# One transformer block with 32 experts: the second weights on a DMA queue of their own

## The chip, the cores and the metric

The kernel runs on one core of a Trainium2 chip. Its time is the device time of one execution in microseconds (us). The engines that matter are TensorE (PE), VectorE (DVE), ScalarE (ACT), GpSimd (POOL) and SyncE (SP, which only issues transfers); 16 DMA engines move data between the memory and the core.

## The reference

One block on 256 tokens of width 1024, all in f32: a modulated mixer (forgetting attention, gated linear attention and pooling side by side), a norm, and a mixture of 32 experts of which each token takes 4, then a last norm. The experts hold nearly all of the bytes: for each expert 1024 x 2048 first weights (gate and up) and 1024 x 1024 second weights (down), 12.6 MB, 403 MB for the 32.

```python
logits = hf @ w_router + b_router
top_logit, top_e = lax.top_k(logits, TOP_K)
gate = jax.nn.softmax(top_logit, axis=-1)
...
def expert_block(args):                       # each expert on the tokens that chose it
    xb, e = args
    gu = xb @ w_gate_up[e] + b_gate_up[e]
    return clamped_swiglu(gu) @ w_down[e] + b_down[e]
...
y = y_rows[dest] * gate
x = layer_norm(DEEPNORM_ALPHA * x + (1.0 + gate2) * y, ln2_g[l], ln2_b[l])
```

## The kernel before

The mixer and the routing take the first 187 us or so; then the experts follow. Each expert has 64 slots for tokens, and two experts make a pair, whose 128 slots fill the partitions.

**Weights.** A ring of 8 slots of 128 x 4096 f32 (2.097 MB each; two pools of 5 and 3 slots) takes the tiles in turn. Expert e has four tiles `g{e}_0` to `g{e}_3` of first weights (`load_up`, L735 to 738) and two tiles `d{e}_0` and `d{e}_1` of second weights (`load_down`, L740 to 743). `load_last` (L745 to 753) brings the second weights of expert 31 in six smaller transfers. The list `jobs` sets the turn: the first weights of e, then the second weights of e - 1; `load_next` takes one. A load may be issued once the tile that stood in its slot has been read by PE, eight tiles earlier: `d0_0` takes the slot of `g0_0`, `d1_0` that of `g1_2`, `g3_0` that of `d0_0`. All of these loads stand in SP's instruction stream and go to one DMA queue.

**One pair.** `dispatch` gathers the tokens with a one-hot matrix on PE (`pxg`), and DVE and ACT scale the result into `xg` (L793 and L791). `gate_up` multiplies `xg` by the four g tiles into `gu`; DVE and ACT make the activation of it (`g` L827, the sigmoid `s` L831 on ACT, `l`). `turned` transposes it (`paT` L839 on PE, `aT` L841 on DVE). `down_sums` multiplies it by the two d tiles into `py`, DVE scales that into `yb` (L857), and `combine` adds the rows of a pair back to the tokens: `ya` on PE, with the gates `sg` (L805, transposed by PE as `psg`, L803). The `py` of an expert is written behind the gate-up of the next.

**Order.** All engines' instructions are put in order by a scheduler, from the program as written. The order on each engine is then fixed, and an engine waits at an instruction until what it needs is there. `mm` at L134 records nearly all matmuls, so that they share one line.

**The barrier.** Ahead of expert 12 the program reads a count and branches (`more_slots`, L868 to 870), for the case that an expert has more than 64 tokens; it isn't taken here. All engines branch, and SP waits there until the loads in flight have landed.

**The end.** `py30` makes `yh` (L998), and `ya` takes it in; then expert 31's second weights, `pyl` and `yl` (L1016), and the last norm.

Of the kernel before, what the change touches and what calls it, by code (L numbers as in the profile page):

```python
# [18 lines left out]
P = 128  # L19
# [93 lines left out]
def block_kernel(ctx: ExitStack, tc, x, w_ada, w_in, gla_w_a2, pool_w, w_out, w_router, w_gate_up, b_gate_up,  # L113
                 w_down, b_down, cols, biases, rows, consts, out):
    nc = tc.nc
    V, A, G, T, SY = nc.vector, nc.scalar, nc.gpsimd, nc.tensor, nc.sync
# [5 lines left out]
    def ring_tile(name):  # L122
        i = 0
        if len(rings) > 1:
            i = int(turn[0] % (NA + NB) >= NA)
            turn[0] += 1
        return rings[i].tile([P, 4096], F32, tag="w", name=name)
# [51 lines left out]
    with tc.tile_pool(name="early", bufs=1) as ea, tc.tile_pool(name="late", bufs=1, side="right") as la_, \  # L179
# [86 lines left out]
        for i, ks in enumerate(((0, 1, 2, 6), (7, 3, 4, 5))):  # L266
            t = ring_tile(f"wo{i}").rearrange("p (k n) -> p k n", n=D)
            for j, k in enumerate(ks):
                wo[k] = t[:, j]
            j, k = (0, 0) if i == 0 else (1, 3)  # L270
            SY.dma_start(t[:, j:j + 3], w_out[0, k * P:(k + 3) * P, :].rearrange("(k p) n -> p k n", p=P))
            j, k = (3, 6) if i == 0 else (0, 7)
# [205 lines left out]
        for t in range(TT):  # L478
            n = (t + 1) * P
# [100 lines left out]
        for a in range(2):  # L580
            for n in range(3):
                t, r0 = n // 2, (n % 2) * CH
# [10 lines left out]
        for t in range(TT):  # L593
# [7 lines left out]
            for h in range(GH):  # L601
                hv = slice(h * GV, (h + 1) * GV)
                mm(po[:, hv], at[:, h], z_gv[:, t, hv], True, False)
                for cc in range(2):
                    n = 2 * t + cc
# [48 lines left out]
        for t in range(TT):  # L654
# [16 lines left out]
            for q in range(2):  # L671
                b = bank(f"ph{t}{q}").rearrange("p (j s) -> p j s", j=4)
                for j in range(4):
                    k = 4 * q + j
                    T.transpose(b[:, j], twos(n1[:, t], k), ident)
                for j in range(4):
                    k = 4 * q + j
# [61 lines left out]

    def load_down(e, i):  # L740
        t = ring_tile(f"d{e}_{i}").rearrange("p (k n) -> p k n", n=D)
        SY.dma_start(t, w_down[0, e, i * 512:(i + 1) * 512, :].rearrange("(p k) n -> p k n", p=P))
        return [t[:, k] for k in range(4)]

    def load_last(e, i):  # L745
# [207 lines left out]
    for e in range(NE):  # L953
        i, m = divmod(e, 2)
# [49 lines left out]
    e, aT, _ = waiting.pop()  # L1004
# [67 lines left out]
```

## Time and profile before

| | us |
|---|---|
| median of 3 runs | 1126.15 |
| lowest and highest run | 1125.25, 1128.42 |
| the profiled execution | 1123.95 |
| its span in the profile | 1122.2 |
| PE busy | 1029.0 (92%) |
| DVE, ACT, POOL busy | 317.3, 98.7, 40.3 |

The span is the profiled execution without what lies around it (1.75 us). Busy shares are means over the mixer, the experts and the end, which have different limits. The mean rate of all transfers is 401 GB/s over the span.

### The profile page before, as it was taken

What the parts mean: (1) busy time and instruction counts of PE and PEld (TensorE: products, weight loads), DVE (VectorE), ACT (ScalarE), POOL (GpSimd) and SP (SyncE); (2) the same over time, 40 slices, a digit from 0 to 9 for tenths busy, and PEclk for the clock granted to TensorE, in tenths of its full rate; (3) what the DMA queues carried; (4) which work ended last, traced back from release to release, by engine and by line L of the source; (5) the groups of instructions that cost most, each with busy time, mean ns of one, the idle gap of its engine ahead of it and who ended that gap; (6) DMA issues with size and microseconds to landing.
All of it is one profiled execution on the core that took longest, in us unless ns stands there. A gap on an engine that the chain in (4) does not pass through costs nothing.

```text
span 1122.2 us, 11042 instructions
## 1 busy us (share of the span) xinstructions
PE 1029.0 (92%) x4734; PEld 434.1 (39%) x4735; DVE 317.3 (28%) x588; ACT 98.7 (9%) x205; POOL 40.3 (4%) x42
## 2 busy tenths in 40 slices
PE   6999989999999999996999999989989898989895
PEld 3656535433333333333344343423333333333221
DVE  1459693322122112211122221213221121211113
ACT  1024121100010000000000000000000000001000
POOL 2170100000000000000000000000000000000000
PEclk9999998999999999998999999999999999999998
DMA  9997599999999999999899999999999999999993
GB/s 321 346 383 290 209 395 382 429 423 426 429 428 425 428 428 427 428 427 424 341 429 427 427 427 428 427 428 428 426 428 428 427 428 427 429 426 427 428 417 118
DMA packets 52998, 449.49 MB, mean 401 GB/s; under 512 B 5056, under 2 KB 18768, under 8 KB 28496
## 3 DMA queue, kind: packets, MB, share of 16 engines
q1 hardware_dynamic: 52320, 447.90, 96.2%
q8 instruction: 39, 0.64, 0.2%
q10 hardware_dynamic: 624, 0.83, 0.2%
q14 instruction: 15, 0.12, 0.0%
HBM read 447.67 MB, written 1.05 MB: 400 GB/s over the span
## 4 chain that ended last, share of the span: by engine, by line
PE 26%; DMA 25%; DVE 1%; issue 1%; DVEq 0%; POOLq 0%; ACT 0%
DMA d<-in_w_down 22%; PE gu L134 12%; PE py L134 6%; PE pxg L134 4%; PE ya L134 3%; DMA g<-in_w_gate_up 3%; PE pyl L134 1%; PE paT L839 1%; DVE aT L841 0%; DVE yb L857 0%; DVE res L921 0%; PE pl L134 0%; DVE yl L1016 0%; DVE st L1020 0%; DVE r L1033 0%
## 5 line engine op out<-in xcount | busy, mean ns | idle before, releaser
L134 PE MATMUL gu<-g,xg 128*64 128x512 f32 x2048 | 462.3, 595 | 12.1 <-DMA g<-in_w_gate_up 10.2
L134 PEld LDWEIGHTS gu<-g,xg 128*64 128x64 f32 x2048 | 143.4, 137 | 292.6 <-issue 261.2
L134 PE MATMUL py<-d,aT 128*64 128x512 f32 x992 | 225.8, 596 | 15.1 <-DMA d<-in_w_down 13.7
L827 DVE TENSOR_SCALAR g<-gu 128x512 f32<-128x512 f32 x32 | 22.1, 691 | 409.7 <-PE gu L134 409.7
L134 PEld LDWEIGHTS py<-d,aT 128*64 128x64 f32 x992 | 70.0, 137 | 150.6 <-issue 137.8
L134 PE MATMUL pxg<-pp,n 128*128 128x128 f32 x512 | 76.7, 301 | 15.1 <-DVE aT L841 7.0
L134 PEld LDWEIGHTS pxg<-pp,n 128*128 128x128 f32 x512 | 68.9, 207 | 43.1 <-issue 29.7
L857 DVE TENSOR_TENSOR yb<-py,g2p 64x512 f32<-64x512 f32 x60 | 41.3, 689 | 133.4 <-PE py L134 132.7
L134 PE MATMUL ya<-yb,sg_None 128*128 128x512 f32 x120 | 58.0, 607 | 5.6 <-DVE yb L857 5.6
L831 ACT ACTIVATE s<-g 128x512 f32<-128x512 f32 x32 | 20.1, 630 | 457.9 <-DVE g L827 457.8
L793 DVE TENSOR_SCALAR xg<-pxg,hA,hB 128x128 f32<-128x128 f32 x64 | 25.8, 409 | 98.9 <-PE pxg L134 89.7
L791 ACT ACTIVATE xg<-pxg,hB,hA 128x128 f32<-128x128 f32 x64 | 28.7, 457 | 273.2 <-DVE xg L793 272.6
L134 PE MATMUL pz<-wz,hT 128*128 128x512 f32 (+2 forms) x128 | 52.4, 547 | 0.0
L841 DVE COPY aT<-paT 128x512 f32<-128x512 f32 x32 | 22.1, 691 | 48.1 <-PE paT L839 48.1
L169 POOL TENSOR_TENSOR rsb<-rtb,half 128x2 f32<-128x2 f32 x1 | 0.7, 699 | 949.1 <-DVE rtb L168 949.1
L134 PEld LDWEIGHTS ya<-yb,sg_None 128*128 128x128 f32 x120 | 20.4, 189 | 28.8 <-issue 17.4
L134 PEld LDWEIGHTS pz<-wz,hT 128*128 128x128 f32 x128 | 23.4, 190 | 17.3 <-issue 14.1
L134 PE MATMUL py<-wo,oT 128*128 128x512 f32 x64 | 29.0, 598 | 0.2 <-ACT oT L642 0.2
L839 PEld LDWEIGHTS paT<-kc,l 128*128 128x128 f32 x128 | 18.0, 209 | 25.3 <-DVE l L833 14.6
L839 PE MATMUL paT<-kc,l 128*128 128x128 f32 x128 | 23.7, 308 | 0.0
L134 PE MATMUL pqk<-hT,wz 128*128 128x256 f32 x96 | 22.3, 382 | 0.8 <-DVE hT L332 0.7
L833 DVE TENSOR_TENSOR l<-l,s 128x512 f32<-128x512 f32 x32 | 22.1, 691 | 3.4 <-DVE l L832 0.5
(244 smaller groups left out, 509.8 us busy)
## 6 DMA issues: line engine op xcount, KB each, us to landing
g<-in_w_gate_up SPq DMA_DIRECT2D x128, 2048.0 KB, 30.4
d<-in_w_down SPq DMA_DIRECT2D x62, 2048.0 KB, 30.4
adam<-in_w_ada SPq DMA_DIRECT2D x4, 2048.0 KB, 16.7
adag<-in_w_ada SPq DMA_DIRECT2D x4, 2048.0 KB, 8.5
ada<-in_w_ada SPq DMA_DIRECT2D x6, 1024.0 KB, 11.2
wz<-in_w_in SPq DMA_DIRECT2D x8, 760.0 KB, 9.7
wo<-in_w_out SPq DMA_DIRECT2D x2, 1536.0 KB, 10.2
ada<-in_w_ada SPq DMA_DIRECT2D x4, 512.0 KB, 7.6
```

Of the source, the lines that this page charges most:

```text
L134: T.matmul(o, l, r, start=start, stop=stop, skip_group_check=True, **kw)
L169: G.tensor_tensor(o, t[:, :n], half[:, :n], op=OP.pow)
L791: A.activation(xg[:, k], bs[k // 4][:, k % 4], AF.Identity, bias=hB[:, k:k + 1], scale=hA[:, k:k + 1])
L793: V.tensor_scalar(xg[:, k], bs[k // 4][:, k % 4], hA[:, k:k + 1], hB[:, k:k + 1], op0=OP.mult, op1=OP.add)
L827: V.tensor_scalar(g, gu[:, 0], LIMIT, None, op0=OP.min)
L831: A.activation(s, g, AF.Sigmoid, scale=SW_ALPHA)
L833: V.tensor_mul(l, l, s)
L839: T.transpose(b[:, j], act[:, j::4], ident)
L841: V.tensor_copy(aT, b)
L857: V.tensor_mul(yb[m * CAP:(m + 1) * CAP, n * 512:(n + 1) * 512], b[r], g2p[r, n * 512:(n + 1) * 512])
```

## The change

In `load_down` the transfer is issued by ScalarE (`A`) in place of SyncE (`SY`), so it goes to ScalarE's own DMA queue. This concerns the two d tiles of experts 0 to 30, 62 transfers of 2.097 MB. `load_up` and `load_last` are as they were.

```diff
     def load_down(e, i):
         t = ring_tile(f"d{e}_{i}").rearrange("p (k n) -> p k n", n=D)
-        SY.dma_start(t, w_down[0, e, i * 512:(i + 1) * 512, :].rearrange("(p k) n -> p k n", p=P))
+        A.dma_start(t, w_down[0, e, i * 512:(i + 1) * 512, :].rearrange("(p k) n -> p k n", p=P))
         return [t[:, k] for k in range(4)]
```

The scheduler puts the transfers among ScalarE's instructions, and it also moves instructions of PE. Three places show it. A name's last number is the buffer's; `x8` counts equal rows in a row.

Place 1, ScalarE around experts 1 and 2, before:

```order
L831 ACTIVATE s_1_1214<-g_1_1210 128x512
L791 ACTIVATE xg1_1221<-pxg1_0_1222,hB_67,hA_66 128x128
L791 ACTIVATE xg1_1221<-pxg1_1_1223,hB_67,hA_66 128x128
L791 ACTIVATE xg1_1221<-pxg1_0_1222,hB_67,hA_66 128x128
L791 ACTIVATE xg1_1221<-pxg1_1_1223,hB_67,hA_66 128x128
L805 COPY sg1_None_1338<-psg1_1335 128x256
L831 ACTIVATE s_2_1328<-g_2_1324 128x512
```

and now:

```order
L831 ACTIVATE s_1_1214<-g_1_1210 128x512
L791 ACTIVATE xg1_1221<-pxg1_0_1222,hB_67,hA_66 128x128
L791 ACTIVATE xg1_1221<-pxg1_1_1223,hB_67,hA_66 128x128
L791 ACTIVATE xg1_1221<-pxg1_0_1222,hB_67,hA_66 128x128
L791 ACTIVATE xg1_1221<-pxg1_1_1223,hB_67,hA_66 128x128
L742 DMA d1_0_1340<-in_w_down 128x4096
L742 DMA d1_1_1342<-in_w_down 128x4096
L742 DMA d2_1_1459<-in_w_down 128x4096
L831 ACTIVATE s_2_1328<-g_2_1324 128x512
L805 COPY sg1_None_1338<-psg1_1335 128x256
L742 DMA d2_0_1457<-in_w_down 128x4096
```

The transfers of `d1` and the second of `d2` now stand on ScalarE behind `s_1` and the four `xg1`, ahead of `s_2`.

Place 2, PE around the last gate-up tile, before (`gu31` is the gate-up of expert 31, `ya` takes in a pair's rows):

```order
L134 MATMUL gu31_4964<-g31_3_4962,xg15_4791 64x512 x8
L134 MATMUL py30_5025<-d30_0_5021,aT30_4954 64x512 x8
L839 MATMUL paT31_5042<-kc_63,l_31_5003 128x128 x4
L134 MATMUL py30_5025<-d30_1_5023,aT30_4954 64x512 x8
L134 MATMUL pyl0_5062<-d31_0_5059,aT31_5047 64x512
L134 MATMUL ya0_1055<-yh_5049,sg15_0_4924 128x512 x2
L134 MATMUL ya1_1056<-yh_5049,sg15_0_4924 128x512 x2
```

and now:

```order
L134 MATMUL gu31_4964<-g31_3_4962,xg15_4791 64x512 x8
L803 MATMUL psg15_5012<-kc_63,pg15_5009 128x128 x2
L134 MATMUL ya0_1055<-yb14_4643,sg14_None_4703 128x512 x2
L134 MATMUL ya1_1056<-yb14_4643,sg14_None_4703 128x512 x2
L134 MATMUL py30_5025<-d30_0_5021,aT30_4954 64x512 x8
L134 MATMUL py30_5025<-d30_1_5023,aT30_4954 64x512 x8
L839 MATMUL paT31_5042<-kc_63,l_31_5003 128x128 x4
```

The first half of `py30` stood behind `g31_3` directly, with `paT31` between the halves; now `psg15` and the `ya` of pair 14 stand between `g31_3` and `py30`, and `paT31` behind both halves.

Place 3, PE between the gate-up of experts 23 and 24, before:

```order
L134 MATMUL gu23_4116<-g23_3_4114,xg11_3955 64x512 x8
L134 MATMUL py22_4199<-d22_0_4195,aT22_4106 64x512 x8
L839 MATMUL paT23_4218<-kc_63,l_23_4155 128x128 x4
L803 MATMUL psg12_4282<-kc_63,pg12_4279 128x128 x2
L134 MATMUL py22_4199<-d22_1_4197,aT22_4106 64x512 x8
L134 MATMUL gu24_4234<-g24_0_4226,xg12_4164 64x512 x8
L134 MATMUL gu24_4234<-g24_1_4228,xg12_4164 64x512 x8
```

and now:

```order
L134 MATMUL gu23_4116<-g23_3_4114,xg11_3955 64x512 x8
L134 MATMUL pxg12_0_4165<-pp12_4161,n1_65 128x128 x4
L134 MATMUL pxg12_1_4166<-pp12_4161,n1_65 128x128 x4
L134 MATMUL pxg12_0_4165<-pp12_4161,n1_65 128x128 x4
L134 MATMUL pxg12_1_4166<-pp12_4161,n1_65 128x128 x4
L134 MATMUL ya0_1055<-yb10_3796,sg10_None_3856 128x512 x2
L134 MATMUL ya1_1056<-yb10_3796,sg10_None_3856 128x512 x2
L134 MATMUL gu24_4234<-g24_0_4226,xg12_4164 64x512 x8
L134 MATMUL gu24_4234<-g24_1_4228,xg12_4164 64x512 x4
L134 MATMUL py22_4199<-d22_0_4195,aT22_4106 64x512 x8
L134 MATMUL py22_4199<-d22_1_4197,aT22_4106 64x512 x8
L839 MATMUL paT23_4218<-kc_63,l_23_4155 128x128 x4
```

`py22`, the second product of an even expert, moves from behind `gu23` to behind `pxg12`, the `ya` of pair 10, and a tile and a half of `gu24`.

## Rows read from the trace of the kernel before

**Rows 1.** The page's 40 slices: busy share of DMA in tenths, and GB/s.

```profile
DMA  9997599999999999999899999999999999999993
GB/s 321 346 383 290 209 395 382 429 423 426 429 428 425 428 428 427 428 427 424 341 429 427 427 427 428 427 428 428 426 428 428 427 428 427 429 426 427 428 417 118
```

**Rows 2.** Windows: us, busy PE, PEld, DVE, ACT, POOL (instructions), PEclk, DMA share, GB/s.

```profile
702.96:761.76 58.80, 53.44 (x251) 20.49 (x251) 12.01 (x23) 3.46 (x8) 0.00 (x0) 1.00 1.01 427
187.00:220.00 33.00, 33.00 (x164) 14.01 (x160) 9.05 (x15) 1.90 (x4) 0.00 (x0) 1.00 0.98 409
218.00:224.00 6.00, 4.66 (x31) 2.91 (x31) 2.91 (x8) 1.72 (x4) 0.00 (x0) 1.00 1.00 426
540.00:550.00 10.00, 8.93 (x40) 3.02 (x38) 3.58 (x7) 1.00 (x2) 0.00 (x0) 1.00 0.53 187
546.77:548.60 1.83, 1.83 (x11) 0.98 (x12) 0.69 (x1) 0.00 (x0) 0.00 (x0) 1.00 0.65 125
548.60:550.60 2.00, 2.00 (x12) 0.72 (x10) 0.00 (x0) 0.00 (x0) 0.00 (x0) 1.00 0.81 303
```

**Rows 3.** Waits of SP over the span: line, waited for, us, times, longest.

```profile
SPq L737 <- PE gu L134: 275.6, 62, 7.4
SPq L737 <- PE py L134: 245.5, 55, 9.7
SPq L742 <- PE gu L134: 232.5, 58, 23.8
```

**Rows 4.** The page's DMA issues: count, KB each, median us from issue to landing.

```profile
d<-in_w_down SPq DMA_DIRECT2D x62, 2048.0 KB, 30.4
```

**Rows 5.** Waits of PE for weights from 560 to 1095 us.

```profile
PE py L134 <- DMA d<-in_w_down: 12.5, 10, 1.3
PE gu L134 <- DMA g<-in_w_gate_up: 10.2, 11, 1.3
```

**Rows 6.** Timeline of ACT, 170 to 224 us: start, us, instruction, idle before.

```profile
175.67 0.34 ACTq L733 DMA_DIRECT2D bdn<-in_b_down  x1
...
220.67 1.39 ACT L791 ACTIVATE xg<-pxg,hB,hA 128x128 f32<-128x128 f32 x3 [0.49 <-DVE xg L793]
```

**Rows 7.** Timeline of PE, 214 to 230 us.

```profile
216.15 4.04 PE L134 MATMUL pxg<-pp,n 128*128 128x128 f32 x32
221.53 7.09 PE L134 MATMUL py<-d,aT 128*64 128x512 f32 x32 [1.34 <-ACT xg L791]
```

**Rows 8.** Timeline of PE, 505 to 550 us.

```profile
510.19 3.70 PE L134 MATMUL ya<-yb,sg_None 128*128 128x512 f32 x8 [0.79 <-DVE yb L857]
...
543.36 0.44 PE L803 MATMUL psg<-kc,pg 128*128 128x128 f32 x2
```

**Rows 9.** Timeline of PE at the end, 1075 to 1122 us.

```profile
1079.49 7.04 PE L134 MATMUL gu<-g,xg 128*64 128x512 f32 x32
...
1092.71 3.65 PE L134 MATMUL py<-d,aT 128*64 128x512 f32 x16 [0.64 <-DMA d<-in_w_down]
1096.19 1.02 PE L134 MATMUL pyl<-d,aT 128*64 128x512 f32 x2
1097.15 2.71 PE L134 MATMUL ya<-yh,sg 64*128 64x512 f32 x8
```

**Rows 10.** Timeline of SP's issues, 186 to 600 us.

```profile
212.82 3.76 SPq L742 DMA_DIRECT2D d<-in_w_down  x2
225.23 11.46 SPq L737 DMA_DIRECT2D g<-in_w_gate_up  x4
...
546.77 0.82 SPq L742 DMA_DIRECT2D d<-in_w_down  x2
```

**Rows 11.** The chain that ended last: start, us, what.

```profile
1056.95 35.72 DMA d<-in_w_down
```

**Rows 12.** DMA queues from 179 to 183 us: packets, MB, share (q10 is ScalarE's).

```profile
q1 hardware_dynamic: 92, 1.25, 90.1%
q10 hardware_dynamic: 48, 0.13, 10.0%
```

## The prediction

> **What bounds the kernel now.** I read the forty slices of the page first. From slice 8 to slice 38 the DMA share is 9 tenths or more and the rate 423 to 429 GB/s, with one exception, slice 20; lower are only the first seven slices and the last two [rows 1]. One pair of experts in the steady part shows the rest: in 58.80 us the DMA share is 1.01 at 427 GB/s while PE is busy for 53.44 [rows 2]. A pair is 12 tiles of 128 x 4096 f32 (2.097 MB), so a tile costs 2.097/0.427 = 4.91 us and a pair 58.9 us. The stream of weights is the bound and PE has 5.4 us to spare in each pair.
>
> Next, who waits. SP waited 275.6 + 245.5 + 232.5 = 753.6 us for PE, always for a ring slot that PE had not yet read [rows 3]. A load of second weights landed 30.4 us after its issue [rows 4], which is 30.4/4.91 = 6.2 tiles: some six tiles always stand in the queue, and a few microseconds of delay at the issue do not reach the transfers. PE waited for weights 12.5 + 10.2 = 22.7 us after the barrier, never longer than 1.3 us at once [rows 5]. So in the steady part neither the order of issue nor the queue decides anything, as long as the queue never runs dry. What a change of queue can move lies at the places where the queue is short: the first experts, the barrier around `more_slots`, and the end.
>
> **The change, part by part.**
>
> (a) *Issue cost.* 62 instructions leave SP and go to ACT. On ACT one DMA issue took 0.34 us [rows 6], so 62 x 0.34 = 21 us of ACT's time, on an engine that is busy 3.46 of 58.80 us per pair [rows 2]. It is hidden by ACT's idle time. On SP nothing is won, since SP stands waiting for PE anyway.
>
> The Trainium skill has a rule against the change here: "DMA: Bandwidth & Descriptors", section "Issuing engines are not separate DMA queues", says that transfers begun by different engines run on the same 16 DMA engines and interleave, and that several issuing engines save only the time of issue. By that rule alone nothing would move in either direction; the rows show that there is no issue time to save, which agrees.
>
> (b) *Steady part.* The ACT issues stand behind ACT's activations. The second weights of an odd expert come behind the sigmoid and the first half of the next `xg`, which makes them some 5 us late; the queue holds 30 us. Even experts' second weights wait for a slot that the same expert's gate-up frees, as before. The moved rows of PE (place 3 of the order: an even expert's `py` now behind `pxg`, `ya` and one and a half tiles of the next gate-up) release the `d` slots about 4.0 + 3.7 + 1.5 x 3.5 = 13 us later [rows 7 to 9], which with the 5 us is again under 30. Cost taken: 0. The cover is the queue of six tiles; where it is gone, each microsecond that a pair runs dry costs some 15 us over the program, which is part of the "more" case below.
>
> (c) *First experts.* Six tiles, `d0_0`, `d0_1` and `g2_0` to `g2_3`, stand in the queue from about 187 us. By 220.00 the window had moved 409 x 33.0 = 13.50 MB [rows 2]; the six are 12.58 MB, so they were done 0.92/0.427 = 2.1 us before its end, at 217.9. Before, SP issued `d1_0` and `d1_1` at 212.82, and the rate stayed at 426 GB/s from 218 to 224 [rows 2, 10]. Now place 1 of the order puts both behind `s_1` and all four `xg1` on ACT, of which the last ends at 220.67 + 1.39 = 222.06 [rows 6]. SP cannot fill in: `g3_0` takes the slot of `d0_0`, which `py0` frees; it was issued at 225.23 [rows 10], and `py0` is no earlier now. How long the transfers need after an issue into an empty queue is seen behind the barrier: SP issued at 546.77, and by 550.60 there were 125 x 1.83 + 303 x 2.00 = 835 KB moved [rows 2, 10]. That is 2.0 of the 3.8 us at 427 GB/s, so the start lies 1.9 us behind the issue. New start 222.1 + 1.9 = 224.0 against 217.9: **+6.1 us** in which nothing moves, on a stream that bounds the rest. Bounds: 0, if PE's own slack at this point or the deeper queue later swallows it (it cannot be regained in a stream at full rate, so this is unlikely), and 8, if the ACT issues come one by one.
>
> (d) *Barrier.* Here SP waits until all loads in flight have landed, and 540 to 550 moved 187 GB/s, a loss of 10 x (1 - 187/428) = 5.6 us [rows 2]. After, two of the eight tiles are issued behind the branch instead of ahead of it, and the next `d12_0` follows on ACT. I find about the same gap: **0**, bounds -1 and +2.
>
> (e) *The end.* This is the largest term. In the single queue the last tile ahead of expert 31's second weights is `d30_1`: the chain ends a transfer at 1056.95 + 35.72 = 1092.67 [rows 11], and PE then owes one half of `py30` (3.65) and begins the `ya` from `yh` at 1097.15, that is 4.44 us after the start of that half at 1092.71 [rows 9]. With two queues `d30_0` and `d30_1` travel beside `g31` on their own queue, which holds two tiles where SP's holds four, so they are through first and the last tile is `g31_3`. How two queues share is seen once in this trace: ACT's `bdn` was issued at 175.67 [rows 6] while SP's stream had more to do; in 179 to 183 48 packets of ACT's queue went beside 92 of SP's [rows 12]. So the small transfer did not stand behind the backlog, and the two alternate.
>
> The Trainium skill tells it so: in "DMA: Bandwidth & Descriptors", section "Queues, rings and completion order", each DMA engine goes round the queues that have work, packet by packet. The row above agrees; for a 2 MB tile no run here shows it yet.
>
> After `g31_3` has landed, PE still owes by place 2 of the order: the last gate-up tile 7.04/2 = 3.52, `psg` 0.44, the `ya` of pair 14 3.70, both halves of `py30` 7.09, and 0.8 for DVE's `yh` as before (1096.36 to 1097.15), with `paT31` beside it: together 15.6 us to the same `ya` [rows 7 to 9]. Difference 15.6 - 4.44 = 11.1; and two `pyl` matmuls which used to fill the gap at 1096.19 now stand behind that `ya`, 2 x 3.65/16 = 0.5. Before, all of this ran while `d30` was on its way. **+11.6 us.** Bounds: +2 if `d30_1` still lands last (the rival below), +15 if the landing of `g31_3` is delayed by a further tile's part of `d31`.
>
> Sum: 6.1 + 0 + 11.6 = 17.7 us. On the profiled execution: 1123.95 + 17.7 = 1141.7. The median of the runs lies 2.2 us above the profiled one, 1126.15 + 17.7 = **1143.9 us**.
>
> **The rivals.**
>
> *Served in order of issue.* If the 16 engines take the transfers as they were issued, `d30_1` remains last. Then (c) stays, and at the end PE has `gu31`, `psg` and `ya` done when `d30_1` lands, but both halves of `py30` run close together with `paT31` behind them: about +2. 1126.15 + 6.1 + 2.1 = 1134. Against it speaks `bdn` [rows 12], for it that `bdn` is small.
>
> *No change.* If the gap in (c) is filled and the end is as before, the stream is the same bytes at the same rate: 1126.  For it: SP's 753.6 us of waiting [rows 3], where nothing is saved by a second issuer. Against it: places 1 and 2 of the order are fixed in the program. The rule of the Trainium skill under (a) ("DMA: Bandwidth & Descriptors", "Issuing engines are not separate DMA queues") would give this time too.
>
> *Faster.* One mechanism: two queues in alternation move more bytes per second than one. Place: the stream from 187 to 1101 us, some 913 us. Price: each 1% of rate gives 9 us. To cancel the 17.7 it must rise from 427.5 to 427.5 x 913/(913 - 17.7) = 436 GB/s; above that the change wins. For 440, 27 - 17.7 = 9 us, so 1117. Against: no slice of the forty is over 429 [rows 1], with the DMA share at 1.01 [rows 2].
>
> The Trainium skill gives, in "DMA: Bandwidth & Descriptors", section "Specifications", a ceiling of 435 GB/s into SBUF; an estimate from it is at most 16 us of gain, short of the 17.7.
>
> *More than forecast.* Two queues in alternation lower the rate by 1% (+9 us), or the slots that (b) releases late leave the queue dry for 1 us in each pair (+15): with a margin, 1152 to 1165.
>
> **How the numbers follow.** My forecast, 1137 to 1150: 0.60. In order of issue, 1131 to 1137: 0.16. No change: 0.09. More: 0.10. Faster: 0.05. The range leaves out no change, faster and half of more, 0.19 together, and goes from 1129 (the gap of (c) at half) to 1157. A difference of 0.3%, 3.4 us, is about what a measurement of this kernel can tell from no change. Slower by more than that takes 0.60, 0.16 but for 0.02, and 0.10: 0.84; within it 0.09 + 0.02 = 0.11; faster 0.05.
>
> **What would show it.** Right: a window between 218 and 224 us that moves little, then 427 GB/s; a pair in the steady part at 58.8 us as before; a chain whose last long transfer is a `g` tile, followed by `gu`, `psg`, `ya`, `py` on PE for some 16 us before the `ya` from `yh`. Wrong: a pair longer or shorter than 58.8 us (the rate changed, or slots run dry), PE waiting for `d` at the end as before, or a rate of 426 from 218 to 224.

## The result, and the profile after

The changed kernel took 1145.66 us (median of 4 runs, 1142.91 to 1148.65), against 1127.29 us for the kernel before in the same comparison: 1.0155 times as long, 95% interval 1.0121 to 1.0189, or 18 us more. The prediction was 1143.9 us.

The profiled execution took 1145.82 us with a span of 1144.1, that is 21.9 us more than the span before. Not all of this is the change. The first sigmoid of the experts (`s` of expert 0 on ScalarE) lies ahead of anything that the change delays. It began here, in the timeline of ACT of the kernel before:

```profile
198.43 0.63 ACT L831 ACTIVATE s<-g 128x512 f32<-128x512 f32 x1 [11.91 <-DVE g L827]
```

and here in that of the changed kernel, which also shows the late issue of `d1`:

```profile
202.08 0.63 ACT L831 ACTIVATE s<-g 128x512 f32<-128x512 f32 x1 [6.38 <-DVE g L827]
...
220.63 0.63 ACT L831 ACTIVATE s<-g 128x512 f32<-128x512 f32 x1 [16.35 <-DVE g L827]
223.38 0.46 ACT L791 ACTIVATE xg<-pxg,hB,hA 128x128 f32<-128x128 f32 x1 [2.12 <-DVE xg L793]
224.32 1.40 ACT L791 ACTIVATE xg<-pxg,hB,hA 128x128 f32<-128x128 f32 x3 [0.48 <-DVE xg L793]
225.32 0.82 ACTq L742 DMA_DIRECT2D d<-in_w_down  x2
```

3.65 us were lost in the mixer, where the instructions are the same. One window there (us, busy time of PE, PEld, DVE, ACT and POOL, granted clock of TensorE, DMA share, GB/s) shows a clock of 0.66, so the engine ran part of it at 1.2 in place of 2.4 GHz; the kernel before had 1.00 in this window:

```profile
120.00:130.00 10.00, 9.97 (x34) 5.04 (x33) 4.81 (x13) 0.00 (x0) 0.00 (x0) 0.66 0.49 195
```

In all traces of this study the first sigmoid starts somewhere between 198 and 207 us. To compare traces I therefore use the stretch from it to the end of the span: 1122.2 - 198.43 = 923.8 us before, 1144.1 - 202.08 = 942.0 us after. The difference, 18.2 us, agrees with that of the medians (18.4).

Where they lie, the windows of the changed kernel tell (same columns as [rows 2]):

```profile
866.53:925.29 58.76, 53.79 (x251) 20.68 (x251) 11.65 (x22) 3.24 (x7) 0.00 (x0) 0.97 1.01 427
218.00:220.00 2.00, 2.00 (x9) 0.61 (x6) 0.09 (x1) 0.00 (x0) 0.00 (x0) 1.00 0.98 418
220.00:222.00 2.00, 2.00 (x18) 2.00 (x18) 1.89 (x3) 0.63 (x1) 0.00 (x0) 1.00 0.85 360
222.00:224.00 2.00, 2.00 (x18) 1.85 (x18) 1.22 (x3) 0.46 (x1) 0.00 (x0) 1.00 0.06 25
224.00:226.00 2.00, 2.00 (x10) 0.77 (x8) 1.41 (x5) 1.26 (x3) 0.00 (x0) 1.00 0.00 0
226.00:230.00 4.00, 4.00 (x22) 2.55 (x20) 0.00 (x0) 0.00 (x0) 0.00 (x0) 1.00 0.94 324
540.00:550.00 10.00, 5.11 (x19) 3.77 (x18) 1.70 (x8) 0.00 (x0) 0.00 (x0) 0.67 0.60 219
550.00:560.00 10.00, 10.00 (x48) 5.75 (x49) 1.94 (x6) 1.72 (x4) 0.00 (x0) 0.82 0.79 303
```

- *The steady part* is as it was: a pair in 58.76 us at 427 GB/s, as in [rows 2].
- *The first experts.* From 220 to 230 us the stream falls short of 427 GB/s by 0.3 + 1.9 + 2.0 + 1.0 = 5.2 us.
- *The barrier.* 540 to 560 us fall short by 4.9 + 2.9 = 7.8 us, against 5.6 before (there 550 to 560 moved 428 GB/s). The second dip has its reason in the timelines of SP and ACT from 540 to 560 us. Behind the branch SyncE issues two tiles; the next load is ScalarE's `d12_0`, which takes the slot of `g12_0`, and PE has read that tile only by 557.4 (its `gu` of expert 12 begins at 553.75):

```profile
544.58 0.82 SPq L737 DMA_DIRECT2D g<-in_w_gate_up  x2
557.45 0.34 ACTq L742 DMA_DIRECT2D d<-in_w_down  x1
```

- *The end*, from the timeline of PE (start, length, instruction, idle time before it):

```profile
1103.07 3.65 PE L134 MATMUL gu<-g,xg 128*64 128x512 f32 x16 [1.04 <-DMA g<-in_w_gate_up]
1106.65 0.44 PE L803 MATMUL psg<-kc,pg 128*128 128x128 f32 x2
1106.93 3.60 PE L134 MATMUL ya<-yb,sg_None 128*128 128x512 f32 x8
1110.46 7.09 PE L134 MATMUL py<-d,aT 128*64 128x512 f32 x32
1117.48 0.75 PE L839 MATMUL paT<-kc,l 128*128 128x128 f32 x4
1118.33 3.37 PE L134 MATMUL ya<-yh,sg 64*128 64x512 f32 x8
```

The last tile waited for is `g31_3`, and from there to the `ya` from `yh` it takes 1118.33 - 1103.07 = 15.3 us, where it took 4.44 from the last half of `py30` [rows 9]. From that `ya` to the end it is 25.8 us in place of 25.05. Together 11.5 us.

5.2 + 2.2 + 11.5 = 18.9 us, 0.7 more than the two traces differ by.

Two more views say what two queues do to the stream. The page's list of issues (count, KB each, median us from issue to landing) has now

```profile
g<-in_w_gate_up SPq DMA_DIRECT2D x128, 2048.0 KB, 25.4
d<-in_w_down ACTq DMA_DIRECT2D x62, 2048.0 KB, 14.3
```

where both kinds landed after 30.4 us before [rows 4]: the second weights overtake. And in a stretch with work in both queues (packets, MB, share of the 16 engines; 250 to 262 us) the packets are divided evenly:

```profile
q10 hardware_dynamic: 175, 2.61, 50.9%
q1 hardware_dynamic: 171, 2.51, 49.1%
```

The Trainium skill says in "DMA: Bandwidth & Descriptors", section "Queues, rings and completion order", that each DMA engine goes round the queues with work packet by packet; the even counts agree, now with tiles of 2 MB. The other rule weighed in the prediction, of the Trainium skill's "DMA: Bandwidth & Descriptors", section "Issuing engines are not separate DMA queues", agrees with this case in that the stream became no faster. It also says that several issuing engines save only time of issue, and here the order of landing and the time of the kernel changed as well.

The time that PE waits for weights changed its form. From 230 us on it was 10.2 us in 11 waits for g and 13.7 in 11 for d before, none over 1.3 us; now there is one line (total, times, longest), for g alone:

```profile
PE gu L134 <- DMA g<-in_w_gate_up: 56.4, 23, 7.2
```

### The profile page after: what moved, and what is told of

The parts are those of the page before. It is cut to its first block, busy times and chain, and to the rows that moved or that the text cites. A ratio compares the mean times of both kernels' runs of the same rounds, so it can differ in the third digit from the quotient of the medians.

```text
span 1144.1 us, 11054 instructions
## 1 busy us (share of the span) xinstructions
PE 1049.0 (92%) x4734; PEld 444.5 (39%) x4735; DVE 313.7 (27%) x588; ACT 96.0 (8%) x205; POOL 40.3 (4%) x42
## 4 chain that ended last, share of the span: by engine, by line
PE 30%; DMA 21%; DVE 1%; issue 0%; DVEq 0%; POOLq 0%; ACT 0%
DMA g<-in_w_gate_up 21%; PE gu L134 15%; PE py L134 7%; PE pxg L134 3%; PE ya L134 3%; PE pyl L134 1%; PE paT L839 1%; PE psg L803 0%; DVE st L1020 0%; DVE r L1033 0%; DVEq L1068 0%; POOLq L1068 0%; ACT r L1038 0%; DVE yl L1016 0%; DVE yh L998 0%
## 5 line engine op out<-in xcount | busy, mean ns | idle before, releaser
L134 PE MATMUL gu<-g,xg 128*64 128x512 f32 x2048 | 490.0, 617 | 58.4 <-DMA g<-in_w_gate_up 56.4
L134 PEld LDWEIGHTS gu<-g,xg 128*64 128x64 f32 x2048 | 150.6, 141 | 348.7 <-issue 272.9
L134 PE MATMUL py<-d,aT 128*64 128x512 f32 x992 | 221.5, 597 | 1.5 <-DVE aT L841 1.5
L134 PEld LDWEIGHTS py<-d,aT 128*64 128x64 f32 x992 | 72.9, 138 | 137.0 <-issue 134.1
L134 PE MATMUL pxg<-pp,n 128*128 128x128 f32 x512 | 69.7, 298 | 4.9 <-DVE pp L781 3.7
L134 PEld LDWEIGHTS pxg<-pp,n 128*128 128x128 f32 x512 | 66.3, 209 | 17.8 <-issue 17.4
L134 PE MATMUL ya<-yb,sg_None 128*128 128x512 f32 x120 | 54.2, 594 | 0.8 <-DVE yb L857 0.8
L793 DVE TENSOR_SCALAR xg<-pxg,hA,hB 128x128 f32<-128x128 f32 x64 | 24.7, 406 | 24.2 <-PE pxg L134 23.3
L134 PEld LDWEIGHTS ya<-yb,sg_None 128*128 128x128 f32 x120 | 21.6, 190 | 24.1 <-issue 21.9
L134 PEld LDWEIGHTS pz<-wz,hT 128*128 128x128 f32 x128 | 23.4, 190 | 17.3 <-issue 14.3
L134 PE MATMUL gu<-bg,sel 96*64 96x512 bf16 x128 | 24.1, 380 | 0.0
## 6 DMA issues: line engine op xcount, KB each, us to landing
g<-in_w_gate_up SPq DMA_DIRECT2D x128, 2048.0 KB, 25.4
d<-in_w_down ACTq DMA_DIRECT2D x62, 2048.0 KB, 14.3
```

The costliest lines, as they stand in the source:

```text
L134: T.matmul(o, l, r, start=start, stop=stop, skip_group_check=True, **kw)
L793: V.tensor_scalar(xg[:, k], bs[k // 4][:, k % 4], hA[:, k:k + 1], hB[:, k:k + 1], op0=OP.mult, op1=OP.add)
```

## The experiments

All of them change the one line of `load_down`, in which an expression in e, or GpSimd, takes the place of `A`. Each was timed beside the kernel before; its medians in the comparisons were 1126.5 to 1126.7 us, with single runs from 1123 to 1133. Ratios are to the kernel before. The last column is the stretch from the first sigmoid to the end in the profiled execution.

| second weights on ScalarE | median, us | ratio (95% interval) | first sigmoid to end, us |
|---|---|---|---|
| none (before) | 1126.7 | 1 | 923.8 |
| all 62 (the change) | 1145.7 | 1.0155 (1.0121 to 1.0189) | 942.0 |
| all but expert 1 | 1141.2 | 1.0116 (1.0081 to 1.0152) | 938.5 |
| all but expert 30 | 1142.7 | 1.0133 (1.0097 to 1.0169) | 935.5 |
| all but experts 1 and 30 | 1135.2 | 1.0080 (1.0054 to 1.0107) | 932.1 |
| all but experts 28 to 30 | 1139.0 | 1.0079 (1.0043 to 1.0114) | 930.8 |
| all but experts 1 and 26 to 30 | 1132.8 | 1.0027 (1.0002 to 1.0052) | 924.6 |
| only expert 1 | 1131.7 | 1.0047 (1.0021 to 1.0073) | 928.1 |
| only experts 28 to 30 | 1137.0 | 1.0092 (1.0064 to 1.0119) | 933.8 |
| only expert 12 | 1124.2 | 0.9975 (0.9954 to 0.9995) | 923.2 |
| none, all 62 on GpSimd | 1143.4 | 1.0133 (1.0093 to 1.0173) | 939.2 |

The intervals of three kernels (expert 1, expert 30, all on GpSimd) overlap that of the change, 1.0121 to 1.0189. For these the times alone don't show a gain, and what is said of where it lies rests on one trace each. The ratio isn't the quotient of the medians; where they differ most (1.0079 against 1138.96/1126.51 = 1.0111, and 1.0027 against 1132.82/1126.51 = 1.0056) a difference of medians is good to some 4 us only.

**Expert 1 back on SyncE.**

```diff
-        A.dma_start(t, w_down[...])
+        (SY if e == 1 else A).dma_start(t, w_down[...])
```

> Expert 1's two second-weight loads go back to SyncE; the other 60 stay on ScalarE. Theory A (the time is lost at three places: some 5 us where the stream runs dry between 222 and 227 us, some 11 us at the end, some 2 us at the barrier, and nothing along the stream): the dry stretch ahead of expert 2's weights is gone (it was 5.2 us in the trace of the changed kernel), and because the order now puts the first two loads of the barrier's eight ahead of the branch again, the barrier gives back up to 2 us more. Expected 5 to 7 us below the changed kernel, about 1139 us, and a rate near 427 GB/s in the stretch that was dry. Theory B (two queues cost a little everywhere, by the rate or by TensorE's lower clock): about 1145 us, since only 2 of 62 loads moved.

4.5 us below the changed kernel by the medians, 3.5 by the traces, where 5 to 7 were expected. The dry stretch is gone:

```profile
220.00:222.00 2.00, 2.00 (x13) 1.19 (x11) 0.99 (x2) 0.26 (x1) 0.00 (x0) 1.00 0.98 418
222.00:224.00 2.00, 2.00 (x19) 2.00 (x19) 1.69 (x3) 0.37 (x1) 0.00 (x0) 1.00 0.95 401
224.00:226.00 2.00, 2.00 (x13) 1.22 (x13) 1.42 (x5) 1.03 (x3) 0.00 (x0) 1.00 1.02 434
...
540.00:550.00 10.00, 5.71 (x27) 5.62 (x28) 1.24 (x7) 0.00 (x0) 0.00 (x0) 0.50 0.82 343
550.00:560.00 10.00, 10.00 (x51) 4.21 (x52) 1.81 (x6) 1.72 (x4) 0.00 (x0) 0.96 0.43 143
```

The barrier gave nothing back: it fell short by 2.0 and 6.65 us, 8.6 in all. So the order of the two tiles ahead of the branch is not what its extra 2 us hang on; that part of the expectation was wrong. Here no load is issued between 531 and 554.87, when ScalarE issues `d12_0`.

**Expert 30 back on SyncE.**

```diff
-        A.dma_start(t, w_down[...])
+        (SY if e == 30 else A).dma_start(t, w_down[...])
```

> Expert 30's two second-weight loads go back to SyncE, the other 60 stay on ScalarE. Theory A: the last tile ahead of expert 31's second weights is d30_1 again. TensorE's order at the end stays that of the changed kernel (psg, the ya of pair 14, both halves of py30 behind the last gate-up), of which all but the last half of py30 fits beside the two d30 transfers. The ya from yh begins about 6 us after d30_1 has landed, against 15.3 us after g31_3 in the changed kernel: 9 to 10 us below the changed kernel, about 1136 us. Theory B: about 1145 us. If the transfers are served in order of issue (rival of the prediction): within 2 us of the changed kernel.

3.0 us below the changed kernel by the medians, 6.5 by the traces (2.0 of them at the barrier, where this run fell short by 5.8 us only, so 4.5 at the end). Expected were 9 to 10: a miss. The timeline of PE at the end tells why:

```profile
1094.26 7.04 PE L134 MATMUL gu<-g,xg 128*64 128x512 f32 x32
1101.22 0.44 PE L803 MATMUL psg<-kc,pg 128*128 128x128 f32 x2
1101.50 3.60 PE L134 MATMUL ya<-yb,sg_None 128*128 128x512 f32 x8
1105.03 7.09 PE L134 MATMUL py<-d,aT 128*64 128x512 f32 x32
```

Nothing here waits for weights; the last such wait in this trace ends at 1042.90, 70 us ahead of the `ya` from `yh`. PE was so far behind the stream that the place of the last tile no longer mattered. In the changed kernel it is nearly so: its wait for `g31_3` is 1.04 us. This gave theory C of the next expectations.

**Experts 1 and 30 back on SyncE.**

```diff
-        A.dma_start(t, w_down[...])
+        (SY if e in (1, 30) else A).dma_start(t, w_down[...])
```

> Both edits together: the second weights of experts 1 and 30 on SyncE, those of 58 loads on ScalarE. Theory A: the gains add, 14 to 17 us below the changed kernel, 1129 to 1132 us, within 0.5% of the kernel before although 58 of 62 loads still go by the second queue. Theory B: above 1140 us.

10.5 us below the changed kernel by the medians, 9.9 by the traces (942.0 - 932.1). Against single edits of 3.5 and 6.5 us in the traces they add, also without the barrier, which fell short by 6.0 us here (4.3 + 4.5 = 8.8 against 8.1). The sum falls short of the 14 to 17 that theory A wanted, mainly because expert 30 alone fell short.

**Only expert 1 on ScalarE.**

```diff
-        A.dma_start(t, w_down[...])
+        (A if e == 1 else SY).dma_start(t, w_down[...])
```

> The kernel before with one edit: only expert 1's two second-weight loads are issued by ScalarE, behind the four xg1. Theory (the issue stands too late at one place and the stream runs dry there, which is never won back): a gap of 5 to 6 us in the transfers between 218 and 226 us and as much in the time, 5 to 6 us above the kernel before. Rival (the gap is swallowed later, because TensorE has 5.4 us to spare in each pair): the gap shows, and the time is within 2 us of the kernel before.

5.2 us above the kernel before by the medians, 4.3 by the traces, and the windows fall short by 1.3 + 2.0 + 1.4 + 0.8 = 5.5 us:

```profile
218.00:220.00 2.00, 2.00 (x19) 2.00 (x18) 1.65 (x4) 0.32 (x1) 0.00 (x0) 1.00 0.35 147
220.00:222.00 2.00, 0.90 (x8) 0.70 (x6) 1.46 (x5) 1.08 (x3) 0.00 (x0) 1.00 0.00 0
222.00:224.00 2.00, 1.76 (x8) 0.63 (x10) 0.48 (x2) 0.65 (x2) 0.00 (x0) 1.00 0.70 131
224.00:226.00 2.00, 2.00 (x12) 0.72 (x10) 0.00 (x0) 0.00 (x0) 0.00 (x0) 1.00 0.69 262
```

Two loads of 190, moved behind four activations, cost 4 to 5 us, and the 900 us of stream that follow win about one back.

**Only experts 28 to 30 on ScalarE.**

```diff
-        A.dma_start(t, w_down[...])
+        (A if e >= 28 else SY).dma_start(t, w_down[...])
```

> The kernel before with only the second weights of experts 28 to 30 issued by ScalarE. Theory C: what is owed at the end is set by the last two or three experts' loads, so nearly all of the end's 11 us appears: 7 to 11 us above the kernel before, 1134 to 1138 us, with g31_3 the last tile that TensorE waits for, or no wait at all. If the debt must build up over many pairs: less than 4 us above.

10.0 us above the kernel before in the traces (933.8 - 923.8), 10.4 by the ratio: six loads at the end cost nearly as much as the end of the changed kernel. But not in the same way. By the waits of PE from 1040 us on (total, times, longest) the engine waits twice for d, and not once for g:

```profile
PE py L134 <- DMA d<-in_w_down: 7.7, 2, 4.2
```

Both waits are for `d29`, and behind each PE runs at a lower clock. The granted clock is 0.58 from 1064.89 to 1071.17 us and 0.55 from 1074.60 to 1081.14, mostly 1.2 in place of 2.4 GHz, and a half that takes 3.65 us in [rows 9] took 6.28 and 6.54:

```profile
1064.89 6.28 PE L134 MATMUL py<-d,aT 128*64 128x512 f32 x16 [4.23 <-DMA d<-in_w_down]
1074.60 6.54 PE L134 MATMUL py<-d,aT 128*64 128x512 f32 x16 [3.43 <-DMA d<-in_w_down]
```

`d29` takes the slots of `g29_2` and `g29_3`, which PE had read by 1033.6 and 1039.6. ScalarE issued both of its tiles behind a copy of its own, 10 us and more later (in the kernel before SyncE issued them from 1026.51 on):

```profile
1049.81 0.37 ACT L805 COPY sg<-psg 128x256 f32<-128x256 f32 x1
1049.89 0.82 ACTq L742 DMA_DIRECT2D d<-in_w_down  x2
```

From the second wait on PE works without a wait for weights, as with expert 30 alone: it is behind the stream, but here because second weights came late, which theory C did not have.

**Experts 28 to 30 back on SyncE.**

```diff
-        A.dma_start(t, w_down[...])
+        (SY if e >= 28 else A).dma_start(t, w_down[...])
```

> The second weights of experts 28 to 30 go back to SyncE, those of 0 to 27 stay on ScalarE. Moving back expert 30 alone had given 3 of the 9 to 10 us that were expected, and its trace showed TensorE at the end without any wait for weights over its last 70 us: it was behind the stream. Theory C (two queues in alternation bring the second weights early and the first weights late, TensorE falls behind the stream by what it owes for the early ones, and this is paid where the stream ends): with six loads back, two pairs of 5.4 us of slack and TensorE's old order at the end, TensorE catches up with the stream; 8 to 11 us below the changed kernel, about 1136 us. Theory A as it was put first (only the last tile's place counts): no more than expert 30 alone gave, 1142 us.

11.2 us less than the changed kernel from the first sigmoid on (942.0 - 930.8), 6.7 by the medians, 8.6 by the ratios; 8 to 11 were expected. The end is that of the kernel before again, with `d30_1` as the last tile, by the timeline of PE:

```profile
1103.84 3.60 PE L134 MATMUL py<-d,aT 128*64 128x512 f32 x16
1107.37 0.74 PE L839 MATMUL paT<-kc,l 128*128 128x128 f32 x4
1108.31 3.65 PE L134 MATMUL py<-d,aT 128*64 128x512 f32 x16 [0.20 <-DMA d<-in_w_down]
...
1112.75 2.71 PE L134 MATMUL ya<-yh,sg 64*128 64x512 f32 x8
```

The wait is 0.20 us, against 0.64 in [rows 9]: with these six loads on SyncE PE has caught up with the stream by the end.

**Experts 1 and 26 to 30 back on SyncE.**

```diff
-        A.dma_start(t, w_down[...])
+        (SY if e == 1 or e >= 26 else A).dma_start(t, w_down[...])
```

> The second weights of experts 1 and 26 to 30 on SyncE, those of the other 25 experts on ScalarE. Theory C: the gap at the start and the debt at the end are both gone, only the barrier's 2 to 3 us remain: 1128 to 1131 us. If two queues cost along the stream (a lower rate, or TensorE's lower clock after its waits): above 1135 us, since 50 of 62 loads still go by the second queue.

924.6 us from the first sigmoid to the end, 0.8 more than before, although 50 loads still go by the second queue. PE waits at the end for the two tiles of `d30` as before, by its timeline:

```profile
1096.75 3.65 PE L134 MATMUL py<-d,aT 128*64 128x512 f32 x16 [1.24 <-DMA d<-in_w_down]
...
1101.72 3.65 PE L134 MATMUL py<-d,aT 128*64 128x512 f32 x16 [0.64 <-DMA d<-in_w_down]
```

The barrier falls short by 5.7 us, about as much as before. The time of the runs is 1.0027 of the kernel before (1.0002 to 1.0052), and the median, 1132.8, lies above the 1128 to 1131 expected; the profiled execution had its first sigmoid at 207.00 us, the latest with one other, so some of that lies ahead of the change. This tells against a cost of two queues along the stream of more than the interval's 6 us: its long waits for g, up to 5.8 us, are there too.

**All second weights on GpSimd's queue.**

```diff
-        A.dma_start(t, w_down[...])
+        nc.gpsimd.dma_start(t, w_down[...])
```

> All 62 second-weight loads are issued by GpSimd in place of ScalarE, so again by a queue of their own; GpSimd has no other work beside the experts, and issues d1_0 as soon as TensorE has read g1_2. TensorE's order is that of the changed kernel but for a few rows. If the start's loss comes from ScalarE's place in its own stream (xg1 ahead of d1) and the end's from the second queue: no dry stretch between 218 and 228 us, the end as in the changed kernel (15 to 16 us from g31_3 to the ya from yh), about 5 us below the changed kernel, 1140 us. If a second queue alone makes the start run dry: 1145 us. If this queue is slower to start or to share: a rate below 425 GB/s along the stream and above 1150 us.

2.2 us below the changed kernel by the medians, 2.8 by the traces. The start runs without a gap, in one window of the same columns:

```profile
218.00:230.00 12.00, 12.00 (x69) 7.54 (x67) 4.61 (x10) 2.35 (x5) 0.82 (x2) 1.00 1.01 429
```

So it is ScalarE's place in its own stream that dries the start, and not the second queue. The barrier fell short by 5.7 us, 2.2 less than in the changed kernel. Of these gains over 3 us went at the end, by the timeline of PE:

```profile
1097.43 6.63 PE L134 MATMUL gu<-g,xg 128*64 128x512 f32 x16 [3.04 <-DMA g<-in_w_gate_up]
...
1115.67 3.37 PE L134 MATMUL ya<-yh,sg 64*128 64x512 f32 x8
```

The last gate-up tile took 6.63 us in place of 3.65, behind a wait of 3.04 us, and the `ya` from `yh` came 18.2 us after its start, in place of 15.3.

**Only expert 12 on ScalarE**, a try for a version faster than both.

```diff
-        A.dma_start(t, w_down[...])
+        (A if e == 12 else SY).dma_start(t, w_down[...])
```

> The kernel before with one edit: the two second-weight loads of expert 12, the first ones behind the barrier, are issued by ScalarE. ScalarE passes the branch without waiting for the transfers, and issues d12_0 when TensorE has read g12_0 (532 us in the trace of before, d12_1 at about 536), while SyncE still waits until 546.8. Theory A: the queue is fed through the barrier, the loss of 5.6 us between 540 and 550 goes away: about 1121.5 us, and 540 to 550 moves more than 400 GB/s. Theory B, or if ScalarE too waits at the branch: no gain, 1127 us or some us more.

The gain expected was 5.6 us. The traces differ by 0.6 us, and the barrier falls short by 3.9 + 1.5 = 5.4 us, as before. ScalarE did not issue `d12_0` when PE had read `g12_0`. By its timeline

```profile
549.73 0.87 ACTq L742 DMA_DIRECT2D d<-in_w_down  x2
550.70 0.63 ACT L831 ACTIVATE s<-g 128x512 f32<-128x512 f32 x1 [17.18 <-issue]
```

and by that of SP

```profile
550.07 10.99 SPq L737 DMA_DIRECT2D g<-in_w_gate_up  x4
```

both engines issue within 0.4 us of each other. ScalarE's first load behind the branch is held back as long as SyncE is. The view of the branch's line, L869, lists ScalarE's `s` with 17.2 us among what waited for it: the load stands at a count that SyncE raises on its way past the branch. No run took that wait away. The timed ratio, 0.9975 with 0.9995 as its upper end, would be a gain of some 3 us, and no row of the trace shows where it would come from. Of the 22 runs of the kernel before beside it six took over 1130 us, of these 12 runs none (1127.55 at most); since the start of the experts alone differs by up to 9 us between traces, I don't count it as a gain.

## Why the prediction was right, point by point

- *(a), issue cost:* right. A pair takes 58.76 us with the issues on ScalarE, as before, so they cost nothing there and nothing was won on SyncE.
- *(b), steady part:* right in what it costs, 0. Long waits of PE for g came in, with a lower clock behind some of them; the kernel with 50 loads on ScalarE (+0.8 us in the trace, at most 1.0052 in the runs) shows that they cost little or nothing as long as the stream goes on.
- *(c), first experts:* 6.1 predicted, 5.2 in the windows. Expert 1 alone reproduces it (4.3 by the traces, 5.2 by the medians), and both expert 1 on SyncE and GpSimd's issue remove the gap.
- *(d), barrier:* 0 predicted with bounds -1 and +2; 2.2 in the trace. The prediction let `d12_0` follow the two late tiles without a gap. But it waits until PE has read `g12_0`, and the queue runs dry a second time. Among the kernels with most second weights on ScalarE the shortfall is 5.7 to 8.6 us. It differs by 2.7 between two kernels whose loads there are issued alike: with expert 1 on SyncE ScalarE issues `d12_0` at 554.87, with experts 1 and 30 on SyncE at 550.75, and in both SyncE's next load comes after it. So it hangs on how far PE is when the branch is passed; no run set that on purpose.
- *(e), the end:* 11.6 predicted, 11.5 in the trace. The sum of the pieces behind `g31_3` was right to 0.3 us (15.6 against 15.3). The reason was too narrow. The prediction took the last tile's place for the cause, and by that reason expert 30 on SyncE had to give back 9 to 10 us. It gave 3 by the medians and 4.5 at the end of its trace. The wider reason that fits: tiles land in another order than the one in which PE takes them, PE waits for one that comes late, and it reaches the end of the stream with a debt of work. In the changed kernel and with GpSimd PE waits for first weights, while second weights land early. With experts 28 to 30 alone the late tiles were those of `d29`; its 10.0 us are of about the same size from another late tile, and don't confirm that early second weights make the debt. Experts 28 to 30 and 26 to 30 back on SyncE show that six loads or more in the old place and order remove it.
- *Two other causes for the end.* One is SyncE's own issue: in the changed kernel SyncE waited 153.8 us in 23 waits for first weights to land before it issued the next ones, where before all waits of its weight loads for landings came to 24.2 us in 28. With GpSimd such waits were 66.3 us in 9, less than half, and yet PE waited 59.0 us in 24 waits for first weights, as much as the 56.4 in the changed kernel. That speaks against it. The other stays open: no run keeps the old order of PE with the second weights of the last experts on a second queue, so what the moved rows (places 2 and 3) add to the debt is not shown.
- *How much was luck.* In the changed kernel the place of the last tile and the debt come out within 1.04 us of each other (PE's wait for `g31_3`), so the number of (e) could not tell them apart. And the terms were off by -0.9 in (c) and +2.2 in (d), in part against each other. The sum, 17.7 against 18.2, agrees better than its terms.
- *The rivals.* Service in the order of issue is out: 175 and 171 packets, and 14.3 against 25.4 us to landing. No change is out by the interval. A faster stream is out at 427 GB/s. A slower stream is out by the same row. In the price of the faster one is a slip: 440 GB/s would save 913 x (1 - 427.5/440) = 25.9 us and not 27, so 1118 us; nothing else hangs on it.

## What to carry to other kernels

In this kernel a second queue added no bandwidth to a stream that already ran at its rate; it changed the order in which things land, by halves. Where the consumer needs the tiles in one order, that order is worth more than a second issuer, above all in the last few tiles, where whatever the consumer has put off is paid in full. And a load that is handed to an engine with work of its own stands behind that work: look for the one place where the queue is short, since of a gap of 5.5 us in the stream that bounds this kernel only about one was won back.

## What the runs showed of the hardware that was not expected

- Between two queues with 2 MB transfers the packets were shared evenly in the stretch shown (50.9% and 49.1% of the engines' time), and the queue with fewer transfers waiting was served far sooner: 14.3 against 25.4 us.
- A wait of a few microseconds can cost TensorE a second time: with GpSimd's issue the tile behind a wait of 3.04 us took 6.63 us in place of 3.65, at a granted clock of 0.55 (mostly 1.2 in place of 2.4 GHz). Behind the 1.04 us in the changed kernel's end it took 3.65, at 1.00.
- The same mixer, instruction for instruction on PE, ended anywhere within 9 us (first sigmoid at 198.43 to 207.01 us), with one cause in view, stretches of lower granted clock: 0.66 between 120 and 130 us in the changed kernel, 0.73 and 0.75 from 120 to 140 in the two latest. A comparison of two traces needs a mark behind such a stretch.
